# One hybrid decoder layer on one Trainium2 core: values transposed beside their keys, a scaling table through another queue, opening products of ones, three later groups

## The chip, the cores and the metric

The kernel runs on one core of a Trainium2 chip. The metric is device microseconds (us) of one execution, the median of three runs. The engines are TensorE (PE in the profile, its weight loads PEld), VectorE (DVE), ScalarE (ACT), GpSimd (POOL) and SyncE (SP, which only starts transfers here). A matmul engine's clock has two levels, 1.2 and 2.4 GHz.

## What is computed

One step of one layer for 512 new prompt tokens and 8 running sequences of 8 tokens, 576 columns in all, in float32:

```python
h = _rmsnorm(x, norm_mix_g)
proj = jnp.einsum('bld,de->ble', h, w_in)
...
o_dn, S_new = _gated_delta_rule(dq, dkk, dvv, g, beta, S0)      # 8 heads, keys and values of 128
h_ml, C_new, n_new, m_new = _mlstm(mq, mk, mv, ig, logf, C0, n0, m0)   # 4 heads
x = x + jnp.einsum('ble,ed->bld', mix, w_out)
u = jnp.einsum('bld,df->blf', _rmsnorm(x, norm_ffn_g), w_up)
x = x + jnp.einsum('blf,fd->bld', silu(gate) * up, w_down)
```

In the gated delta rule a key's norm scales the key and, in this kernel's form, the value too: `irk` is the square root of the sum of the key's squares, and a value, transposed to have tokens on partitions, is multiplied by it. The triangular system of each chunk is solved through the inverse of a unit triangular matrix.

## The kernel before

**Dense products.** All of w_in, w_out, w_up and w_down is multiplied in split precision: a weight tile and an activation tile are each split into a high and a low part (`wh`, `wl`, `ah`, `al`), and each 128x128 weight block takes three products (`three`, L196 to L201) in two halves of 288 columns, six matmuls. `dense` walks 16 blocks k of one output tile; after each k it calls `tick`. Weights come as 512 KB tiles of eight blocks (`raw`), cast to `wh` by ACT (L120) and subtracted to `wl` by DVE (L121).

**Small products.** The heads' work consists of generators. `spawn` puts one on a list, `tick` advances each that is due, and `yield n` makes it wait n ticks, so a small product stands between two k of a dense product. PE's order is the order in which the program is written; the other engines' order is set by a scheduler with priorities. The heads run in the order m0 d0 d1 m1 d2 d3 m2 d4 d5 d6 d7 m3 (d: gated delta, m: mLSTM). Five heads (d1, d3, d5, d6, d7) do their key products while the delta head before them runs its recurrence (L751 to L771) and its sample part (`dn_sample`); d0, d2 and d4 do theirs alone.

**PSUM for small products.** `psr()` (L111) gives one of four banks. A bank is taken again when everything that reads the products in it has run.

**One delta head** (`dn_head`, L660). Keys are transposed (L683) and ACT squares each of four chunks with a running sum (L686) and scales it (L687); a second bank holds the samples' transposed keys (L689) and two small products (L690, L691). POOL turns the sums into `irk` with a power (L696). One tick later come the keys' products (L710), one tick later keys by queries (L721), one tick later the values' transposes (L732) and, in a bank of their own, the samples' values (L737), scaled by `irk` on ACT (L735, L738). Then `inverse` runs on (L918 to L965), and the recurrence.

**The start** (`startup`, L360). `g1`, 16 scaling columns (8 KB), is fetched through POOL's queue; x comes as 16 tiles of 288 KB through SP's queue, with weight tiles after tiles 1, 7 and 15. ACT makes `ah` from x and g1 (L384), DVE makes `al` (L385). `gate_rows` (L429) computes gates in products between the dense ones (L446, L455, L476, L480, L520).

**Line numbers in the change.** A line of the kernel before stands at +1 in the changed kernel up to L372, at +5 up to L679, at +6 for L683 to L691, at +7 for L702, at +8 for L710 to L723, at +7 for L732 and L735, and at +4 from L751 on. L698 and L711 there are the transposes of samples' values and its scaling, which were L737 and L738.

Of the kernel before, what the change touches and what calls it, by code (L numbers as in the profile page):

```python
# [12 lines left out]
AF = mybir.ActivationFunctionType  # L13
ALU = mybir.AluOpType

P = 128
D = 2048
KT = 16
# [20 lines left out]
OPA = 1600  # L39
YI = 8  # L40
YJ = 20


G1, G2, G3, CW, DG, MG, FW, FBI, GB, AL, M0, NPAR = 0, 16, 32, 48, 144, 145, 153, 417, 505, 506, 507, 515
# [22 lines left out]
class Layer:  # L67
# [292 lines left out]
    def startup(self):  # L360
        nc, I = self.nc, self.I
        self.par = self.cp.tile([P, NPAR], F32, tag="par", name="par")
        g1 = self.cp.tile([P, KT], F32, tag="g1", name="g1")
        nc.gpsimd.dma_start(out=g1, in_=I["par"][:, G1:G1 + KT])
        self.ones = self.cp.tile([P, P], F32, tag="ones", name="ones")
        nc.vector.memset(self.ones, 1.0)
        nc.scalar.activation(self.rstd_tile()[:, 0:1], self.ones[:, 0:1], AF.Copy)
        self.eps6 = self.cp.tile([P, 1], F32, tag="eps6", name="eps6")
        nc.vector.memset(self.eps6, EPS)
        self.epsh = self.cp.tile([P, 1], F32, tag="epsh", name="epsh")  # L370
        nc.vector.memset(self.epsh, EPS * EPS * P)

        self.xh, self.xl, self.xs = [], [], []
        self.gw = self.r(shape=[P, KT, 32])
        acts = [self.new_act(k) for k in reversed(range(KT))][::-1]
        for k in range(KT):
            x = self.r()
            self.xs.append(x)
            nc.sync.dma_start(out=x, in_=I["xT"][k])
            if k in (1, 7, 15):  # L380
                self.load_unit()
            hi, lo = acts[k]
            g = g1[:, k:k + 1]
            nc.scalar.activation(hi, x, AF.Copy, scale=g)  # L384
            nc.vector.scalar_tensor_tensor(out=lo, in0=x, scalar=g, in1=hi.bitcast(F32), op0=ALU.mult, op1=ALU.subtract)  # L385
            self.xh.append(hi)
            self.xl.append(lo)
        for k in range(0, KT, 4):
            self.gate_weights(k, g1)
        nc.sync.dma_start(out=self.par, in_=I["par"])  # L390
# [38 lines left out]
    def gate_rows(self):  # L429
        nc, I, O = self.nc, self.I, self.O  # L430
        V, A, Pl, mm = nc.vector, nc.scalar, nc.gpsimd, nc.tensor.matmul
# [34 lines left out]
        for j, (s, _) in enumerate(quarters):  # L466
            Pl.tensor_copy(there[s, :, 0:8], self.ident[s, s].rearrange("p (g w) -> p g w", g=4))
            Pl.tensor_copy(back[s, :, j], self.ident[s, 32 * j:32 * j + 8].unsqueeze(1).to_broadcast([32, 4, 8]))
            n, v = ((3, 0.5), (5, 1.0), (4, 1.0), (5, 1.0))[j]
# [40 lines left out]
        for s, t in quarters:  # L510
            V.scalar_tensor_tensor(out=t5[s, t], in0=y[s], scalar=cq[s, 4:5], in1=val[s], op0=ALU.mult, op1=ALU.add)
        edge.__exit__(None, None, None)
        yield 12
        R1, R2, R3 = self.r(), self.r(), self.r()
        for t in (R1, R2, R3):
            Pl.memset(t, 0.0)
# [68 lines left out]
        for i, t in enumerate((R1, R2, R3)):  # L585
            pr = self.psr()
            pv = pr.rearrange("p (c g w) -> p c g w", c=4, g=4)
# [72 lines left out]
    def dn_head(self, h, q, k, v, sz):  # L660
        nc, I, O = self.nc, self.I, self.O
        V, A, Pl, mm = nc.vector, nc.scalar, nc.gpsimd, nc.tensor.matmul
        sl4 = slice(SEQ, NT)
# [13 lines left out]
        Pl.memset(ss[64:128, 4:5], 1.0)  # L677
        kd = self.r()
        kds = self.t1([64, P], "kds", 2)  # L679
        pk = self.psr()  # L680
        for c in range(NCH):
            sl, n = self.blk(c)
# [5 lines left out]
        pk = self.psr()  # L688
        nc.tensor.transpose(pk[0:64, 0:P], k[:, sl4], self.ident)  # L689
        mm(pk[0:64, P:P + 64], k[:, sl4], k[:, sl4], start=True, stop=True)  # L690
        mm(pk[0:64, P + 64:2 * P], k[:, sl4], q[:, sl4], start=True, stop=True)  # L691
        A.activation(kds, pk[0:64, 0:P], AF.Square, accum_out=ss[0:64, 4:5])
        A.activation(kds, pk[0:64, 0:P], AF.Copy, scale=self.col(2, 4, 1, h))
        V.tensor_scalar(out=ss, in0=ss, scalar1=EPS, scalar2=None, op0=ALU.add)
        irk, cj = self.sm(5, "irk"), self.sm(5, "cj")
# [5 lines left out]
        U, KQ = self.r(), em  # L701
        V.scalar_tensor_tensor(out=U[0:64, sl4], in0=pk[0:64, P:P + 64], scalar=cjc(4), in1=em[0:64, sl4], op0=ALU.mult, op1=ALU.mult)  # L702
        V.tensor_tensor(out=KQ[0:64, sl4], in0=pk[0:64, P + 64:2 * P], in1=em[0:64, sl4], op=ALU.mult)
        yield 1


# [7 lines left out]
        res = []  # L714
        inv = self.inverse(U, res, 0)
        next(inv)
        yield 1
        pr = self.psr()
        for c in range(NCH):
            sl, n = self.blk(c)  # L720
# [4 lines left out]


        vs = self.r()
        vss = self.t1([64, P], "vss", 2)
        pv = self.psr()
        for c in range(NCH):  # L730
            sl, n = self.blk(c)
# [1 line left out]
        for c in range(NCH):  # L733
            sl, n = self.blk(c)
            A.activation(vs[:, sl], pv[:, sl], AF.Copy, scale=irk[:, c:c + 1])  # L735
        pv = self.psr()
        nc.tensor.transpose(pv[0:64, 0:P], v[:, sl4], self.ident)  # L737
        A.activation(vss, pv[0:64, 0:P], AF.Copy, scale=irk[0:64, 4:5])  # L738

        yield YI  # L740
        yield from inv
# [111 lines left out]
    def inverse(self, U, res, more):  # L853
# [44 lines left out]
        def masked(i):  # L898
            m = U if i == len(LV) - 1 else self.r()
            Pl.tensor_tensor(out=c4(m), in0=c4(U), in1=self.bc4(self.con[:, C_LV + P * i:C_LV + P * i + P]), op=ALU.mult)  # L900
            return m

        m = masked(0)
        yield YJ + more
        self.tc.cur_priority -= PR
# [166 lines left out]
    def ml_sample(self, h, caug, kws, sT, gl, finish):  # L1072
        nc, O = self.nc, self.O
        V, A, Pl, mm = nc.vector, nc.scalar, nc.gpsimd, nc.tensor.matmul
        sl = slice(SEQ, NT)
        yield 2
        qc = self.r(shape=[P, 2, 257])
        for g in range(2):
            pr = self.psr()
            for j in range(4):  # L1080
                mm(pr[32 * j:32 * j + 32, 0:257], self.qim[:, 4 * g + j], caug[g][:, j], start=True, stop=True)
            A.copy(qc[:, g], pr[:, 0:257])
        yield 2
        pn = self.psr()
        mm(pn[0:64, 0:257], sT[0:64, sl], self.vas, start=True, stop=False)
        for g in range(2):
            mm(pn[32 * g:32 * g + 32, 0:257], self.pick[:, 0], qc[:, g], start=False, stop=True)
        fin = self.spawn(finish(pn, 4))
        bmk = self.con[0:64, C_BM:C_BM + NB]
        yield 4  # L1090
        pm = self.psr()
        mm(pm[:, 0:NB], kws, bmk, start=True, stop=True)
        for b in range(NB):
            n1 = caug[b // 4][:, b % 4, 256:257]
            V.scalar_tensor_tensor(out=n1, in0=n1, scalar=gl[:, 4 + b:5 + b], in1=pm[:, b:b + 1], op0=ALU.mult, op1=ALU.add)
        kp = self.pack(kws, P, "kp", ("hhl", "hhl"))
        vp = self.pack(self.vas, 256, "vp", ("hlh", "lhh"))
        for g in range(4):
            vm = self.masked_rows(vp, g // 2, g % 2 * 2, 2)
            yield W  # L1100
            pr = self.psr()
            mm(pr, kp[:, g // 2], vm, start=True, stop=True)
            for i in range(2):
                b = 2 * g + i
                cc = caug[b // 4][:, b % 4, 0:256]
                V.scalar_tensor_tensor(out=cc, in0=cc, scalar=gl[:, 4 + b:5 + b], in1=pr[:, 256 * i:256 * i + 256], op0=ALU.mult, op1=ALU.add)
        for g in range(2):
            self.later(6, O["sC"][h, g], caug[g])
        while not fin[3]:
            yield 1  # L1110
# [628 lines left out]
```

## Time and profile before

| | us |
|---|---|
| median of three runs | 2661.8 (2661.02 to 2662.45) |
| the profiled execution | 2660.97 |
| its span | 2659.2 |
| PE busy | 2628.2, 99% of the span |
| DVE, ACT, POOL busy | 2057.7, 1083.3, 461.6 |
| first matmul starts | 8.50 |
| share of PE in the chain that ended last | 96% |

The span is the time from the first to the last instruction in the profile; some 1.8 us of the execution lie around it. "Idle before" in a row is the time in which an engine had nothing running, with what ended it behind the arrow. A busy PE is not a PE at its peak, since matmuls overlap: the distance from one start to the next is what counts.

### The profile page before, as it was taken

To read this page: it belongs to the slowest core of one execution; us is meant where nothing else is said; L and a number is where in the kernel's file an instruction comes from. 1 tells how busy PE (TensorE), PEld (TensorE's weight loads), DVE (VectorE), ACT (ScalarE), POOL (GpSimd) and SP (SyncE) were. 2 spreads that over 40 slices of the span, in tenths; PEclk is the share of its full clock that TensorE was granted. 3 is DMA by queue.
4 is the path that set the end of the run, shared out by engine and by line. 5 is a ranking of instruction groups with operands and counts; after the bars stand their busy time and mean duration, and the time that the engine had idled before them with its cause. 6 is when DMAs were issued, how large, how long until landed. Compare 5 with 4: busy or idle time off the path is not lost.

```text
span 2659.2 us, 49165 instructions
## 1 busy us (share of the span) xinstructions
PE 2628.2 (99%) x20061; PEld 2584.9 (97%) x20061; DVE 2057.7 (77%) x3448; ACT 1083.3 (41%) x1697; POOL 461.6 (17%) x670
## 2 busy tenths in 40 slices
PE   8999999999999999999999999999999999999998
PEld 8999999999999999999999999999999999999997
DVE  6676666667765455599999999999999998988656
ACT  5333433434434333244444444444444443434224
POOL 2222322322322001111212222222222200000001
PEclk9999999999999999999999999999999999999999
DMA  5242322422323434343333333333333463342332
GB/s 206 83 126 87 130 84 78 131 86 85 98 85 106 154 121 135 129 137 114 109 109 109 109 108 108 106 108 107 108 108 109 133 231 90 119 137 71 123 98 100
DMA packets 112682, 304.05 MB, mean 114 GB/s; under 512 B 21928, under 2 KB 28216, under 8 KB 112456
## 3 DMA queue, kind: packets, MB, share of 16 engines
q1 hardware_dynamic: 108616, 292.20, 34.2%
q0 software_dynamic: 1600, 6.35, 0.7%
q8 instruction: 157, 2.57, 0.4%
q10 hardware_dynamic: 2240, 2.36, 0.2%
q14 instruction: 69, 0.57, 0.1%
HBM read 262.44 MB, written 38.42 MB: 113 GB/s over the span
## 4 chain that ended last, share of the span: by engine, by line
PE 96%; DVE 2%; ACT 1%; issue 0%; POOL 0%; DMA 0%; DVEq 0%; POOLq 0%
PE pd L200 38%; PE pr L1358 33%; PE pd L1358 13%; PE pr L200 4%; PE pr L1588 1%; DVE r L1623 0%; PE pr L918 0%; PE pr L258 0%; DVE wl L121 0%; PE pr L721 0%; PE pr L758 0%; ACT r L686 0%; PE pr L930 0%; PE pr L1055 0%; ACT r L687 0%
## 5 line engine op out<-in xcount | busy, mean ns | idle before, releaser
L120 ACT CAST wh<-raw 128x1024 fp32r<-128x1024 f32 (+1 forms) x392 | 403.2, 1029 | 732.2 <-PE pd L200 391.6
L1358 PE MATMUL pr<-bh,wl 128*128 128x288 f32 x2248 | 663.3, 295 | 0.9 <-DVE wl L121 0.9
L1358 PE MATMUL pr<-bh,wh 128*128 128x288 f32 x2248 | 663.4, 295 | 0.3 <-ACT wh L120 0.3
L1358 PE MATMUL pr<-bl,wh 128*128 128x288 f32 x2248 | 663.3, 295 | 0.0
L121 DVE TENSOR_TENSOR wl<-raw,wh 128x1024 fp32r<-128x1024 f32 (+1 forms) x392 | 471.3, 1202 | 109.6 <-ACT wh L120 105.5
L200 PE MATMUL pd<-ah,wh 128*128 128x288 f32 x2304 | 512.9, 304 | 8.5 <-ACT wh L120 8.5
L200 PE MATMUL pd<-al,wh 128*128 128x288 f32 x2304 | 492.9, 295 | 0.0
L200 PE MATMUL pd<-ah,wl 128*128 128x288 f32 x2304 | 491.3, 294 | 0.0
L1358 PEld LDWEIGHTS pr<-bh,wl 128*128 128x128 f32 x2248 | 423.0, 188 | 1.9 <-DVE wl L121 1.9
L1358 PEld LDWEIGHTS pr<-bh,wh 128*128 128x128 f32 x2248 | 422.6, 188 | 0.5 <-ACT wh L120 0.5
L1358 PEld LDWEIGHTS pr<-bl,wh 128*128 128x128 f32 x2248 | 422.9, 188 | 0.1
L200 PEld LDWEIGHTS pd<-ah,wh 128*128 128x128 f32 x2304 | 367.1, 188 | 21.0 <-ACT wh L120 8.5
L200 PEld LDWEIGHTS pd<-ah,wl 128*128 128x128 f32 x2304 | 368.8, 188 | 0.3 <-DVE wl L121 0.3
L200 PEld LDWEIGHTS pd<-al,wh 128*128 128x128 f32 x2304 | 368.1, 188 | 0.0
L120 ACT CAST wh<-s 128x1024 fp32r<-128x1024 f32 (+1 forms) x180 | 178.8, 993 | 364.5 <-DVE s L1323 138.4
L1358 PE MATMUL pd<-bh,wl 128*128 128x288 f32 x888 | 262.1, 295 | 0.6 <-DVE wl L121 0.6
L1358 PE MATMUL pd<-bl,wh 128*128 128x288 f32 x888 | 262.2, 295 | 0.0
L1358 PE MATMUL pd<-bh,wh 128*128 128x288 f32 x888 | 262.0, 295 | 0.0
L1240 POOL COPY fst<-r 128x18 f32<-128x18 f32 x88 | 97.6, 1109 | 678.8 <-DVE r L1396 678.8
L121 DVE TENSOR_TENSOR wl<-s,wh 128x1024 fp32r<-128x1024 f32 (+1 forms) x180 | 206.5, 1147 | 6.8 <-ACT wh L120 2.2
L1358 PEld LDWEIGHTS pd<-bh,wl 128*128 128x128 f32 x888 | 167.1, 188 | 0.9 <-DVE wl L121 0.9
L1358 PEld LDWEIGHTS pd<-bl,wh 128*128 128x128 f32 x888 | 167.1, 188 | 0.0
(420 smaller groups left out, 3736.1 us busy)
## 6 DMA issues: line engine op xcount, KB each, us to landing
raw<-in_w_up SPq DMA_DIRECT2D x176, 512.0 KB
raw<-in_w_in SPq DMA_DIRECT2D x112, 512.0 KB
raw<-in_w_down SPq DMA_DIRECT2D x40, 512.0 KB
raw<-in_w_out SPq DMA_DIRECT2D x32, 512.0 KB
raw<-in_w_down SPq DMA_DIRECT2D x40, 384.0 KB
hid<-r SPq DMA_DIRECT2D x44, 288.0 KB
r<-hid SPq DMA_DIRECT2D x40, 288.0 KB
r<-in_xT SPq DMA_DIRECT2D x32, 288.0 KB
```

The source lines that it names most:

```text
L120: self.last_split = (nc.scalar.copy(hi, src), nc.vector.tensor_tensor(out=lo, in0=src, in1=hi.bitcast(F32), op=ALU.subtract))
L121: nc.vector.tensor_tensor(out=lo, in0=src, in1=hi.bitcast(F32), op=ALU.subtract))
L200: mm(outs[hf], w, x[:, hf * HALF:(hf + 1) * HALF], start=first and i == 0, stop=last and i == 2)
L1240: nc.gpsimd.tensor_copy(f, rb[:, 512:602].rearrange("p (b w) -> p b w", b=9)[:, :, 0:2])
L1358: mm(out, w[:, ks], x[:, sl], start=k == 0 and i == 0, stop=k == nk - 1 and i == 2)
L1588: mm(pr[:, 0:n], w[:, ks], acts[kk][:, a * NT + sl.start:a * NT + sl.stop], start=kk == 0 and i == 0, stop=kk == FB - 1 and i == 2)
```

## The change

It has four parts. The opening products: 18 matmuls of a 128x128 tile of ones with itself, whose result nobody reads, stand first on PE. The scaling columns' transfer goes from POOL's queue to ACT's. The samples' values are transposed into the bank of the samples' keys, behind L691, and scaled by ACT once `irk` is there; the bank of their own goes away. Three groups stand later in ticks: L520 by two, L721 (and what follows in its head) by one, L1092 (and what follows in `ml_sample`) by one.

```diff
+NW = 18
...
-        nc.gpsimd.dma_start(out=g1, in_=I["par"][:, G1:G1 + KT])
+        nc.scalar.dma_start(out=g1, in_=I["par"][:, G1:G1 + KT])
...
+        pw = self.psr()
+        for _ in range(NW):
+            nc.tensor.matmul(pw[:, 0:P], self.ones, self.ones, start=True, stop=True)
...
-        yield 12
+        yield 14
         R1, R2, R3 = self.r(), self.r(), self.r()
...
+        vss = self.t1([64, P], "vss", 2)
         pk = self.psr()
...
         mm(pk[0:64, P + 64:2 * P], k[:, sl4], q[:, sl4], start=True, stop=True)
+        nc.tensor.transpose(pk[0:64, 2 * P:3 * P], v[:, sl4], self.ident)
...
         V.tensor_tensor(out=KQ[0:64, sl4], in0=pk[0:64, P + 64:2 * P], in1=em[0:64, sl4], op=ALU.mult)
+        A.activation(vss, pk[0:64, 2 * P:3 * P], AF.Copy, scale=irk[0:64, 4:5])
         yield 1
...
         next(inv)
-        yield 1
+        yield 2
         pr = self.psr()
...
-        pv = self.psr()
-        nc.tensor.transpose(pv[0:64, 0:P], v[:, sl4], self.ident)
-        A.activation(vss, pv[0:64, 0:P], AF.Copy, scale=irk[0:64, 4:5])
...
         bmk = self.con[0:64, C_BM:C_BM + NB]
-        yield 4
+        yield 5
```

PE in head d1, beside the recurrence of d0. Before (a line of dots stands for dense products, and between L689 and L710 for L690 and L691 too; `con` is the identity, r_2100 the key, r_1941 the query, r_2243 the value):

```order
L832 MATMUL pr_2528<-vss_1910,Xs_1876 64x128
L683 MATMUL pr_2553<-con,r_2100 128x128 x4
L689 MATMUL pr_2566<-con,r_2100 64x128
...
L710 MATMUL pr_2588<-r_2100 128x128 x4
...
L762 MATMUL pr_2619<-r_1909,r_1828 128x128
L764 MATMUL pr_2619<-r_1744,S_2455 128x128
L765 MATMUL pr_2619<-r_1746,r_1909 128x128
L721 MATMUL pr_2626<-r_1941,r_2100 128x128 x4
...
L839 MATMUL pr_2639<-r_1746,vss_1910 128x64
L732 MATMUL pr_2646<-con,r_2243 128x128 x4
L737 MATMUL pr_2655<-con,r_2243 64x128
```

The same place in the changed kernel (r_2118 the key, r_1959 the query, r_2261 the value):

```order
L689 MATMUL pr_2551<-con,r_2118 128x128 x4
L695 MATMUL pr_2564<-con,r_2118 64x128
...
L698 MATMUL pr_2564<-con,r_2261 64x128
...
L718 MATMUL pr_2588<-r_2118 128x128 x4
L836 MATMUL pr_2613<-vss_1849,Xs_1898 64x128
...
L766 MATMUL pr_2646<-r_1937,r_1847 128x128
L768 MATMUL pr_2646<-r_1758,S_2479 128x128
L769 MATMUL pr_2646<-r_1760,r_1937 128x128
L729 MATMUL pr_2653<-r_1959,r_2118 128x128 x4
...
L739 MATMUL pr_2667<-con,r_2261 128x128 x4
L843 MATMUL pr_2676<-r_1760,vss_1849 128x64
```

L737 has gone into the keys' group as L698. L721, now L729, stands two k of the dense product behind L718 where there was one between L710 and it, still in one group with the recurrence's three products, and the sample product L832, now L836, has gone from ahead of the keys' transposes to behind L718. In the w_in part the dense products are left for small ones at 268 places, where there were 247: groups of two heads that stood between the same two k now often stand a k apart.

ACT at the same place. Before (left out under the dots: more rows of L686, L687, L692, L693 and two L797):

```order
L833 ACTIVATE vss_1910<-pr_2528,cj_1851 64x128
L797 CAST vp_2538<-vss_1910 32x128 x4
L686 ACTIVATE r_2551,ss_2549<-pr_2553 128x128
...
L687 ACTIVATE r_2551<-pr_2553,cols 128x128
L797 CAST kp_3336<-kds_2552 32x128 x2
L771 COPY r_1744<-pr_2619 128x128
L723 ACTIVATE r_1941<-r_1941 128x576
L842 COPY r_1744<-pr_2639 128x64
L735 ACTIVATE r_2644<-pr_2646,irk_2573 128x128 x4
L738 ACTIVATE vss_2645<-pr_2655,irk_2573 64x128
```

In the changed kernel:

```order
L692 ACTIVATE r_2548,ss_2546<-pr_2551 128x128
...
L693 ACTIVATE r_2548<-pr_2551,cols 128x128
L837 ACTIVATE vss_1849<-pr_2613,cj_1872 64x128
L801 CAST kp_3359<-kds_2549 32x128
L801 CAST vp_2623<-vss_1849 32x128 x4
L801 CAST kp_3359<-kds_2549 32x128 x2
L711 ACTIVATE vss_2550<-pr_2564,irk_2572 64x128
L731 ACTIVATE r_1959<-r_1959 128x576
L775 COPY r_1758<-pr_2646 128x128
L742 ACTIVATE r_2666<-pr_2667,irk_2572 128x128 x4
```

The sample's scaling and its casts (L833 and L797, now L837 and L801) have gone from ahead of the eight instructions on the keys to behind them, and L738, now L711, stands ahead of L771 and L735. On POOL the power (L696, now L703) stood behind two L806 and now stands ahead of them.

## Rows read from the trace of the kernel before

**Rows 1.** The page's part 1: busy us of each engine, share of the span, instructions.

```profile
PE 2628.2 (99%) x20061; PEld 2584.9 (97%) x20061; DVE 2057.7 (77%) x3448; ACT 1083.3 (41%) x1697; POOL 461.6 (17%) x670
```

**Rows 2.** Waits on PE: line, what it waited for, us in total, times, longest.

```profile
PE pd L200 <- ACT wh L120: 8.5, 1, 8.5
PE pr L721 <- ACT r L687: 3.8, 5, 0.8
...
PE pr L737 <- POOL r L866: 0.9, 2, 0.5
...
PE pr L1092 <- DVE hn L1040: 0.7, 2, 0.4
PE pr L520 <- DVE r L511: 0.7, 1, 0.7
...
PE pr L737 <- DVE r L703: 0.4, 1, 0.4
```

**Rows 3.** Timeline of the start: start, us, engine, line, operation, idle before.

```profile
0.84 0.17 DVE L366 MEMSET ones<- 128x128 f32 x1 [0.84 <-PEq L1715]
...
1.52 0.68 POOL L364 DMA_DIRECT2D g<-in_par  x1
...
6.07 1.44 ACT L384 ACTIVATE ah<-r,g 128x576 fp32r<-128x576 f32 x2 [3.83 <-DMA g<-in_par]
```

**Rows 4.** Timeline of PE from its first matmul on; x2 are two matmuls.

```profile
10.41 0.68 PE L200 MATMUL pd<-ah,wh 128*128 128x288 f32 x2
10.89 0.68 PE L200 MATMUL pd<-al,wh 128*128 128x288 f32 x2
...
12.89 0.42 PE L200 MATMUL pd<-ah,wh 128*128 128x288 f32 x2
...
17.12 0.43 PE L200 MATMUL pd<-al,wh 128*128 128x288 f32 x2
```

**Rows 5.** SP's queue: the issue that waited for the second weight tile, and its wait.

```profile
12.28 0.33 SPq L379 DMA_DIRECT2D r<-in_xT  x1
...
SPq L379 <- DMA raw<-in_w_in: 1.0, 1, 1.0
```

**Rows 6.** Timeline of ACT and DVE at the second weight tile and behind it.

```profile
12.37 1.04 ACT L120 CAST wh<-raw 128x1024 fp32r<-128x1024 f32 x1
...
14.00 1.22 DVE L121 TENSOR_TENSOR wl<-raw,wh 128x1024 fp32r<-128x1024 f32 x1
...
15.13 5.92 DVE L385 SCALAR_TENSOR_TENSOR al<-r,g,ah 128x576 fp32r<-128x576 f32 x8
```

**Rows 7.** Timeline of PE in head d1.

```profile
209.22 0.43 PE L832 MATMUL pr<-vss,Xs 64*64 64x128 f32 x2
...
211.56 1.05 PE L710 MATMUL pr<-r 128*128 128x128 f32 x8
212.36 0.51 PE L200 MATMUL pd<-ah,wh 128*128 128x288 f32 x2
212.72 0.42 PE L200 MATMUL pd<-al,wh 128*128 128x288 f32 x2
...
213.24 0.38 PE L762 MATMUL pr<-r,r 128*128 128x128 f32 x2
...
214.82 1.16 PE L721 MATMUL pr<-r,r 128*128 128x128 f32 x8 [0.76 <-ACT r L687]
```

**Rows 8.** Timeline of ACT and POOL in the same stretch.

```profile
210.84 1.04 POOL L806 TENSOR_TENSOR vm<-vp,con 96x512 fp32r<-96x512 f32 x1 [3.72 <-ACT vp L797]
...
211.36 0.28 ACT L686 ACTIVATE r<-pr 128x128 f32<-128x128 f32 x1
...
214.34 1.18 POOL L696 TENSOR_TENSOR irk<-ss,half 128x5 f32<-128x5 f32 x1 [1.13 <-DVE ss L694]
214.40 0.37 ACT L687 ACTIVATE r<-pr,cols 128x128 f32<-128x128 f32 x1
214.79 0.60 ACT L797 CAST kp<-kds 32x128 fp32r<-32x128 f32 x2
```

More of the change, by code (lines that the diff above doesn't have):

```diff
@@ L727, in dn_head @@
         vs = self.r()
-        vss = self.t1([64, P], "vss", 2)
         pv = self.psr()
```

## The prediction

> **What bounds the kernel.** I read the page's busy times first. PE is busy for 2628.2 of the span's 2659.2 us, so only three things can move the end: time in which PE stands, time in which it works at half rate, and instructions added to it [rows 1]. DVE is next with 77% and cannot set the end over the whole span, only in single stretches. So I went to the waits on PE. The reader is to see there that 8.5 us lie ahead of the first matmul and that the other named waits are short and come from few lines: L721 stands five times for ACT's L687, 3.8 us in all; L737 three times, 0.9 and 0.4 us; L1092 twice, 0.7; L520 once, 0.7 [rows 2]. Those four make 6.5 us, and they are the lines that the change moves. Then the timelines of the start: ACT's first `ah` waits 3.83 us for the scaling columns, which POOL had issued at 1.52 [rows 3]. PE begins at 8.50 with a pair of matmuls every 0.48 us (10.41 to 10.89); from 12.89 to 17.12 sixteen pairs take 0.264 us each [rows 4]. 576 columns in 0.48 us are 1.2 GHz; the second pace belongs to 2.4. (The column of granted clock says full speed throughout, so I take the spacing.)
>
> **The opening products and the scaling columns.** What does an earlier and faster start bring? Nine pairs start between 8.50 and 12.89, 4.39 us, where nine at the later pace take 2.4: half rate costs 2.0 us. But PE has to be fed. The ninth block of the first dense product needs the second weight tile and `al` of the ninth x tile. The issue that waits for that weight tile does so for 1.0 us and goes out at 12.28, so the tile lands just before [rows 5]; ACT casts it from 12.37 to 13.41, and nothing in the change brings that forward, since x and weights come in the same order through SP's queue. DVE took `wl` from 14.00, with `al` behind it from 15.13, 0.74 us apiece (5.92 for eight) [rows 6]. In the changed kernel DVE is free sooner and can start `wl` at 13.41: 1.22 and 0.74 later, at 15.4, PE can have the second pair of the ninth block. Before, it had it at 17.12 [rows 4]. From there PE is slower (0.79 a block) than DVE (0.74). So the start gives 17.1 less 15.4, **1.7 us**, if PE gets there in time: 25 pairs at 0.264 lie ahead, so the first one must start by 8.75 at full rate.
>
> Does it? `ones` is ready at 1.01 [rows 3]. Four products of the same kind (L710, eight records) take 0.80 us, 211.56 to 212.36 [rows 7], so 18 take 3.6 us at full rate, or 6.6 at 0.48/0.264 of that: they end between 4.6 and 7.6. The scaling columns need not even come sooner, since 8.50 is early enough; their move only makes room. The issue itself goes ahead of ACT's first work, in a stretch in which ACT waited 3.83 us [rows 3], and POOL loses 0.68 us of work that PE does not wait for; both at nothing.
>
> The clock is the uncertain part. In this trace it rose after 4.4 us of PE's work, which lies inside the time of the ones; by that row the start gives 1.7 and the sum is 7.2. The Trainium skill (TensorE: Matmul & The Clock Gate, Part 1) says that one kernel had 6, 11 or 14 slow products at its start, depending on the run; no run here shows that yet. By that rule the rise may come only after the ones have ended.
>
> If it does, the first real product starts at about 7.6 and the first nine pairs are slow: the ninth block's second pair is at 7.6 + 25 x 0.264 + 2.0 = 16.2, a start worth 0.9 and a sum of 6.4. The bounds of this term: nothing, since even twice 3.6 us of ones ends at 8.2, ahead of the 8.50 of before, which excludes a loss; and 2.9, if DVE's `wl` did not stand ahead of that `al` (1.22). I take 1.7, since the rows give DVE that order.
>
> **L520, two ticks later.** It waited 0.7 us for DVE's L511 [rows 2]. A tick is one block, three pairs, 0.79 us; two are 1.58, twice the wait. What follows in that generator, three later groups and four small transfers on SP's queue, comes 1.6 us later too; the heads wait for them, but the dense products go on meanwhile and the last small product stands some 88 blocks (70 us) ahead of the w_out part, so that costs nothing. Gain **0.7**.
>
> **L1092, one tick later**: it waited twice 0.4 us for its bank; 0.79 covers it. Gain **0.7**, bounds 0 and 1.0 (L1044 behind it had 0.3 of its own).
>
> **Samples' values beside their keys.** The transpose is moved, not removed: the same PE time. What goes is its bank and the wait for it, 0.9 and 0.4 [rows 2]: **1.3**. In return the keys' bank is held until ACT's L711, which needs `irk`. The next to take that bank in a paired head is L732; see below whether it waits.
>
> **L721, one tick later.** Head d1: L721 could have gone at 214.06 and went at 214.82, when the last L687 (214.40, 0.37) had read the bank [rows 7, 8]. One tick alone makes 214.85. In the new order, though, L762 takes that bank, ahead of L721: it stood at 213.24, and comes 0.79 (the tick), 0.2 (the transpose) and 0.4 (L832, which now lies between) later, 214.6 [rows 7]. That would be 0.1 short, but ACT no longer does the sample's scaling and four casts ahead of the keys: at 0.30 a cast (0.60 for two) and 0.3 for the scaling it reaches L687's last 1.2 to 1.5 us sooner, at about 213.4 [rows 8]. So L762 does not wait. Then L732: L762 at 214.6, 0.82 to L721, 0.92 for it (214.82 to 215.74 as before), a block of 0.9: 217.2. L711 behind it: last L687 at 213.4, scaling and seven casts 2.4, L711 0.4: 216.2; the power (214.34, 1.18) comes 1.2 sooner, at 214.3, and does not end last. The cover is **1 us**, and the gain all five waits, **3.8**, bounds 0 and 3.8.
>
> **What the moves add.** PE leaves the dense products at 268 places instead of 247. Behind L710 the first pair takes 0.36 us instead of 0.264 [rows 7], so a place costs at most 0.10; a bound below is nothing, where a group hides its switch. No row has a place by itself, so I take the middle, 0.05: 21 places, **-1.0**, bounds -2.1 and 0.
>
> **Sum.** 1.7 + 0.7 + 0.7 + 1.3 + 3.8 - 1.0 = 7.2 us. The profiled execution took 2660.97, 0.8 under the median of 2661.8; 2660.97 - 7.2 = 2653.8 there, so 2654.6 for the median. A measurement of this kernel can tell about 0.2%, 5.3 us, from no change: the border is 2656.5.
>
> **Rivals.**
> *The ones do not raise the clock in time.* For it: one trace cannot tell how the clock's rise varies. Against: 4.4 us of work were enough there. The sum is 6.4, 2655.4. Chance 0.13.
> *The wait moves on to the bank's next user.* L762 takes the keys' bank, L732 the bank held by L711, and ACT's order behind L687 is longer by L833 and four casts. If ACT is 1.8 us later than I have it, 0.8 us past its cover, the five waits of 0.76 come back under other lines and 7.2 - 3.8 = 3.4 remain: 2658.4. For it: the cover of 1 us is made of sums of rows. Against: ACT is busy 41%. Chance 0.18.
> *Slower.* The same place, but L711 late by more: ACT takes its queue in order, L711 stands behind eight casts and scalings that wait on PE and DVE in turn, and L771 and L735 of the recurrence stand behind it. At 3.5 us late, 2.5 past the cover in five heads, it costs 12.5: 2654.6 + 12.5 = 2667.1. It turns into a loss from 1.4 us past the cover on (7.2/5). For it: POOL's power has already waited 1.13 us for DVE in this stretch [rows 8]. Against: in the new order the power stands ahead of the two L806 (1.04 each) it stood behind. Chance 0.05.
>
> **How the numbers follow.** The forecast of 2654.6 has 0.62, the rivals 0.13, 0.18 and 0.05; 0.02 is for what I do not see. From the forecast, 0.55 lies below the border and 0.07 above (an L721 wait or two left, or switches at 0.10); of the first rival 0.10 lies below. Faster 0.65, within 0.2% 0.30, slower 0.05. The range: below, the term of switches at nothing and L1044's wait gone (1.3 more) and 0.7 for the spread of the runs shown: 2652.6; a start near its upper bound is left to the outer tenths. Above, the second rival: 2658.5. With the slower rival, what lies below and the unseen, under 0.2 is left out.
>
> **What would show it.** Right: 18 products on PE from about 1.1; the pairs at 0.264 from the first one; the ninth block's second pair near 15.4; no row of waits for L737's successor, L729 (L721 before) or L525 (L520 before); PE's idle time down by some 6 us besides the start. Wrong: a row of 0.48 us pairs after 7; new waits of PE for ACT's L693 or L711 near L766 or L739 in the five paired heads; a first dense product that ends no sooner.

## The result, and the profile of the changed kernel

The changed kernel takes 2668.5 us, median of 11 runs, where the kernel before took 2662.0 beside it: a ratio of 1.0025 with a 95% interval of 1.0016 to 1.0033. It is 6.5 us slower; the forecast was 7.2 us faster, with a range up to 2658.5. The profiled execution of the changed kernel took 2666.8, its span 2665.0 (2659.2 before).

**The page first** (busy time of PE, then the chain that ended last).

```profile
PE 2634.2 (99%) x20097; PEld 2590.5 (97%) x20097; DVE 2067.2 (78%) x3448; ACT 1081.0 (41%) x1697; POOL 457.4 (17%) x669
...
PE 88%; DVE 7%; issue 2%; DMA 1%; ACT 1%; POOL 1%; SPq 0%; DVEq 0%; POOLq 0%; ACTq 0%
```

PE's busy time grew by 6.0 us against [rows 1], but the opening products alone are 6.7 of it. What is new stands in the chain: PE had 96% of it and DVE 2%; now PE has 88% and DVE 7%.

**The start** did what was forecast. On PE (start, us, engine, line, operation, idle before):

```profile
1.06 6.67 PE L377 MATMUL pr<-ones 128*128 128x128 f32 x36 [1.06 <-DVE epsh L372]
7.48 0.51 PE L201 MATMUL pd<-ah,wh 128*128 128x288 f32 x2
...
8.96 0.43 PE L201 MATMUL pd<-ah,wh 128*128 128x288 f32 x2
9.22 0.43 PE L201 MATMUL pd<-al,wh 128*128 128x288 f32 x2
...
15.01 0.54 PE L201 MATMUL pd<-al,wh 128*128 128x288 f32 x2
```

and on ACT and DVE:

```profile
3.86 1.44 ACT L389 ACTIVATE ah<-r,g 128x576 fp32r<-128x576 f32 x2 [1.18 <-DMA g<-in_par]
...
11.92 1.05 ACT L121 CAST wh<-raw 128x1024 fp32r<-128x1024 f32 x1 [0.51 <-DMA raw<-in_w_in]
...
13.00 1.23 DVE L122 TENSOR_TENSOR wl<-raw,wh 128x1024 fp32r<-128x1024 f32 x1
```

ACT's first `ah` starts at 3.86 where it had started at 6.07 [rows 3]. The ones fill PE from 1.06 to 7.48, 6.4 us; their 36 records start 0.21 us apart at first and 0.11 apart from 6.1 on, so PE changes to its full pace while they run. Behind them no real pair is at the slow pace: the pairs follow each other at 0.26 us, but for two waits, and the ninth block's second pair stands at 15.01. Before it stood at 17.12 [rows 4]: 2.1 us.

That sets one trace against one trace, and the start is not the same in each. Over all profiled executions, that pair lies between 17.1 and 19.2 in the five without the ones, which begin with 7 to 12 pairs more than 0.35 us apart, and between 14.9 and 16.4 in the nine with them; there the ones change pace between 4.7 and 7.1, always before they end. The means are 2.7 us apart.

**The waits on PE** (line, what it waited for, us in total, times, longest):

```profile
PE pr L762 <- DVE rr L757: 4.1, 5, 0.9
PE pr L850 <- DVE r L730: 3.7, 4, 1.3
PE pr L922 <- DVE r L915: 3.1, 2, 1.5
PE pd L201 <- DVE wl L122: 2.3, 2, 2.0
...
PE pr L766 <- DVE hn L1044: 1.2, 2, 0.6
```

None of the four old lines is left: the 6.5 us of [rows 2] at L721, L737, L1092 and L520 are gone. In their place stand 14 us of waits for one engine, DVE, 10.9 of them in the delta heads (L762, L850, L922). The sum of these two traces closes: PE's gaps of over 50 ns behind the first 20 us went from 10.9 to 17.4 us (summed over all its rows), +6.5; the start gave -2.1; the span grew by 5.8, so 1.4 is left for all else, the 21 more interruptions of the dense products among it.

**Head d1, where L850 waits for KQ's bank.** PE:

```profile
205.36 0.60 PE L689 MATMUL pr<-con,r 128*128 128x128 f32 x4
...
207.31 1.05 PE L718 MATMUL pr<-r 128*128 128x128 f32 x8
208.29 0.43 PE L836 MATMUL pr<-vss,Xs 64*64 64x128 f32 x2
...
218.01 0.47 PE L850 MATMUL pr<-vm,kp 96*128 96x512 f32 x1 [1.12 <-DVE r L730]
```

ACT, POOL and DVE in the same stretch:

```profile
209.54 1.26 ACT L801 CAST vp<-vss 32x128 fp32r<-32x128 f32 x4
...
208.81 1.27 POOL L703 TENSOR_TENSOR irk<-ss,half 128x5 f32<-128x5 f32 x1 [5.94 <-DVE ss L701]
...
213.37 1.04 POOL L810 TENSOR_TENSOR vm<-vp,con 96x512 fp32r<-96x512 f32 x1
214.70 1.04 POOL L810 TENSOR_TENSOR vm<-vp,con 96x512 fp32r<-96x512 f32 x1 [0.29 <-DVE vp L803]
215.70 1.28 POOL L904 TENSOR_TENSOR r<-r,con 128x512 f32<-128x512 f32 x1
...
213.47 1.08 DVE L803 TENSOR_TENSOR vp<-vss,vp 32x128 fp32r<-32x128 f32 x1
...
214.85 2.42 DVE L877 TENSOR_TENSOR r<-r 128x256 f32<-128x256 f32 x1
217.19 0.68 DVE L730 TENSOR_TENSOR r<-pr,r 128x512 f32<-128x512 f32 x1
```

The sample product L836 stands behind the next head's key group (L689 to L718), and so do its casts, and the two masks that POOL makes from them (L810). Before, the masks ran at 210.84 [rows 8] and 212.16, around the keys' products at 211.56 [rows 7]; now they come 6.1 and 7.4 us behind those. There they meet the inverse's additions on DVE: L877, 128x256, starts beside the second L810, lasts 2.42 us through it and through L904 behind it, and ends 0.29 after L904. KQ (L730) stands behind it on DVE, and PE's L850 waits for KQ's bank. The same place before:

```profile
211.05 0.97 DVE L799 TENSOR_TENSOR vp<-vss,vp 32x128 fp32r<-32x128 f32 x1 [0.36 <-ACT vp L797]
...
212.16 1.04 POOL L806 TENSOR_TENSOR vm<-vp,con 96x512 fp32r<-96x512 f32 x1 [0.28 <-ACT kds L692]
...
218.84 1.28 POOL L900 TENSOR_TENSOR r<-r,con 128x512 f32<-128x512 f32 x1
...
218.84 0.67 DVE L722 TENSOR_TENSOR r<-pr,r 128x512 f32<-128x512 f32 x1
219.44 1.29 DVE L873 TENSOR_TENSOR r<-r 128x256 f32<-128x256 f32 x2
```

Here L722 ran ahead of the long addition; that is the first of the two in the last row and took 0.97 us beside L900 alone. In the unpaired heads, with no POOL instruction beside it, the same 128x256 addition takes 0.40 (three times in either kernel). In d0 before, where it is the longest of the line's three (shortest, middle and longest in ns):

```profile
L873 DVE TENSOR_TENSOR r<-r x3: 174/293/404, 153.2 to 155.7; 64x32 f32<-64x32 f32 x1, 128x256 f32<-128x256 f32 x1, 128x128 f32<-128x128 f32 x1
```

In the changed kernel it takes 2.42 us in d1, d3 and d7, beside two masks, and 1.17 in d5 and d6, where only the second L810 lies beside it. The two waits at L922, 1.5 us each, are in d5 and d6.

### The profile page after: what moved, and what is told of

Read it like the earlier page. It is cut to its first block, busy times and chain, and to the rows that moved or that the text cites. A ratio compares the mean times of both kernels' runs of the same rounds, so it can differ in the third digit from the quotient of the medians.

```text
span 2665.0 us, 49244 instructions
## 1 busy us (share of the span) xinstructions
PE 2634.2 (99%) x20097; PEld 2590.5 (97%) x20097; DVE 2067.2 (78%) x3448; ACT 1081.0 (41%) x1697; POOL 457.4 (17%) x669
## 4 chain that ended last, share of the span: by engine, by line
PE 88%; DVE 7%; issue 2%; DMA 1%; ACT 1%; POOL 1%; SPq 0%; DVEq 0%; POOLq 0%; ACTq 0%
PE pr L1362 33%; PE pd L201 32%; PE pd L1362 13%; PE pr L201 3%; PE pr L1592 1%; DVE wl L122 1%; DVE r L625 0%; DVE bl L122 0%; DVE r L877 0%; DVE vp L803 0%; DVE r L894 0%; DVE r L896 0%; ACT wh L121 0%; DVE r L1627 0%; DMA r<-ud 0%
## 5 line engine op out<-in xcount | busy, mean ns | idle before, releaser
L122 DVE TENSOR_TENSOR wl<-raw,wh 128x1024 fp32r<-128x1024 f32 (+1 forms) x392 | 472.0, 1204 | 95.6 <-ACT wh L121 90.6
L122 DVE TENSOR_TENSOR wl<-s,wh 128x1024 fp32r<-128x1024 f32 (+1 forms) x180 | 206.5, 1147 | 6.3 <-ACT wh L121 1.1
```

The lines of the kernel that those rows point to most:

```text
L122: nc.vector.tensor_tensor(out=lo, in0=src, in1=hi.bitcast(F32), op=ALU.subtract))
```

## The experiments

Theory A: the tick at the keys-by-queries products (yield 2 before L729) is the cost, since the rest of its head slips against the next. Theory B: the merged bank is the cost. Theory C: it takes both. Later A1 and A2 part: A1 says that the slip of the sample part does it, A2 that the products' own lateness does. Each kernel has its own line numbers; I give the counterpart where it isn't plain. Ratios stand to the kernel before on the same chip, five rounds each.

### The start alone

The 18 products of ones and the scaling columns' queue, as in the change, on the kernel before.

> The kernel before with the two parts of the start alone: the 18 products of ones and the scaling columns on ScalarE's queue. Every theory gives the same here: in the profile of the changed kernel the ninth block's second pair stood 2.1 us earlier and no pair ran slowly, so 2.1 us less than before (2659.9 us by a median of 2662.0), the waits in the mixer as before. Were the products of ones to cost something later (another clock, another order), the rest of the kernel would be longer and the gain under 1 us.

Measured: 2659.8 by 2661.4 of before, ratio 0.9993 (0.9985 to 1.0002). 1.7 us less, of the size expected, though the interval holds no change as well.

### The merged bank alone

```diff
+        vss = self.t1([64, P], "vss", 2)
...
         mm(pk[0:64, P + 64:2 * P], k[:, sl4], q[:, sl4], start=True, stop=True)
+        nc.tensor.transpose(pk[0:64, 2 * P:3 * P], v[:, sl4], self.ident)
...
+        A.activation(vss, pk[0:64, 2 * P:3 * P], AF.Copy, scale=irk[0:64, 4:5])
         yield 1
...
-        vss = self.t1([64, P], "vss", 2)
...
-        pv = self.psr()
-        nc.tensor.transpose(pv[0:64, 0:P], v[:, sl4], self.ident)
-        A.activation(vss, pv[0:64, 0:P], AF.Copy, scale=irk[0:64, 4:5])
```

> The kernel before with the transposition of the sample's values beside the keys alone (one bank and one wait fewer, the scaling of them earlier on ScalarE). Theory A (the tick that puts the key-by-query products later is what costs): the wait of 1.3 us in three heads goes, 0 to 1.3 us less than before, no wait for DVE. Theory B (the merged bank is held until the scaling is read from it, and this puts the heads late): the waits for L757's, L730's and L915's counterparts on DVE appear here, and the time is 6 to 10 us more than before.

Measured: 2662.6 by 2661.4, ratio 1.0005 (0.9996 to 1.0014). Theory B falls: none of the waits of the paired heads appears. But the gain isn't there either. On PE (L917 is the inverse's first product, L918 before, in the unpaired heads d0, d2 and d4):

```profile
PE pr L724 <- ACT r L688: 3.6, 5, 0.7
PE pr L917 <- issue: 2.3, 3, 0.8
```

and on DVE and POOL in d0:

```profile
176.51 1.80 DVE L908 TENSOR_TENSOR r<-cx,con 128x512 f32<-128x512 f32 x1
...
178.36 0.69 DVE L910 STREAM_TRANSPOSE r<-r 128x512 f32<-128x512 f32 x1
...
175.98 1.77 POOL L899 TENSOR_TENSOR r<-r,con 128x512 f32<-128x512 f32 x1
```

The 1.3 us at L737 went, and 2.3 came some 25 us on in the same three heads. The profile names no releaser, but L917 starts at 179.16, 0.1 after the transposition it needs. PE came there sooner, and DVE, which runs without a break through this stretch, did not. Part of DVE's time there is due to POOL: L908 lies beside the mask L899, takes 1.80 us and ends 0.55 after it, where its counterpart takes 0.68 with no mask beside it (L913 in d5 of the changed kernel). Those 1.1 us were there before too (1.79); only now PE is early enough to wait for them.

### The tick at the products alone

```diff
         next(inv)
-        yield 1
+        yield 2
```

> The kernel before with the key-by-query products one tick later (yield 2 for yield 1 at L721's group) alone. Theory A: the five waits at L721 (3.8 us) go, and the waits for DVE that the changed kernel shows (some 13 us) come, as the sample part of the head before now lies behind the next head's key group: 8 to 11 us more than before, about 2671 us. Theory B: only the 3.8 us go, about 2658 us. Theory C (it takes two of the parts together): under 4 us more or less than before.

Measured: 2678.0 by 2661.4, ratio 1.0062 (1.0049 to 1.0075). Theory A's direction, and some 6 us more than its upper end; B and C fall. On PE:

```profile
PE pr L839 <- ACT r L771: 9.6, 5, 2.0
PE pr L758 <- DVE rr L753: 6.5, 3, 2.4
```

The five waits at L721 are gone, and the long addition takes up to 2.4 us as in the changed kernel. The largest wait is one that the changed kernel does not have: L839, the sample's next product, wants a bank that ACT's L771 has still to read, and L771 waits for DVE's `S` (L768) behind an addition and a cast's difference that take 1.0 and 1.1 us beside POOL's work (0.17 and 0.28 alone). In the changed kernel L839's counterpart L843 goes at 213.22, ahead of L771's counterpart (214.97), so it takes another bank there; the wait comes at L850 instead, 3.7 us. That the bank that is no longer taken shifts the ring of four is the likely reason, which no run shows by itself. The changed kernel without the start's 2.1 us would be 8.6 above before, where the tick alone is 16.6: beside it the other parts are worth some 8 us, without it next to nothing (the changed kernel with the old tick, below).

### The changed kernel with the old tick there

The change as it is, but `yield 1` before the products.

> The changed kernel with yield 1 again at the key-by-query products, all else as changed. Theory A: 2.1 (start) + 1.3 (the bank) + 0.7 + 0.7 (the two other groups) = 4.8 us less than before, about 2657 us, no waits for DVE in the heads, and the five waits at L721 (3.8 us) back. Theory B: still slower than before, by 6 to 10 us. Theory C: between the two, with part of the waits for DVE left.

Measured: 2658.8 by 2661.4, ratio 0.9990 (0.9981 to 0.9999): Theory A, some 2 us above its number. The waits for DVE in the paired heads are gone. It is short of 2657 mainly by 3.0 us of waits at L922, the inverse's first product, as in the run of the merged bank.

### The products' tick, given back behind them

In the changed kernel, and in the kernel before with `yield 2` at the products:

```diff
-        yield YI
+        yield YI - 1
         yield from inv
```

On the changed kernel:

> The changed kernel, with the tick that the key-by-query products were put later given back behind the values' transpositions (yield YI - 1 there), so that the next head and this head's sample part stand to each other as before. Theory A1 (not the products' own lateness costs, but that the sample part of one head slips by a tick against the next head's key group): the waits for DVE in the paired heads go and those at the products stay away: 2668.5 less 8 to 13 us, 2656 to 2660 us, and at least 2 us under the run with yield 1. Theory A2 (the products' own tick makes KQ late, and with it the bank): the waits for KQ at the sample's state products stay, 3 to 4 us of them, above 2662 us.

Measured: 2657.2 by 2661.5, ratio 0.9983 (0.9974 to 0.9992). On the kernel before:

> The kernel before with the key-by-query products one tick later and the tick given back (yield 2, then yield YI - 1), nothing else. Theory A1: the five waits at L721 (3.8 us) go and nothing comes: about 2657.6 us by a before of 2661.4. Theory A2: some 3 to 10 us more than that. A rival to both: the wait of 0.75 us only moves to the next that wants a bank or ScalarE in the same place (L839 or L732): 2660 to 2661.5 us.

Measured: 2660.8 by 2661.5, ratio 0.9998 (0.9988 to 1.0007). A1 holds in both: the products are as late as in the changed kernel, and neither L850 nor L762 waits; in the first the long addition still takes 1.50 us beside POOL's L904, but KQ has run ahead of it. So the contention is not gone; nothing of weight stands behind it. On PE in the second:

```profile
PE pr L721 <- ACT r L771: 2.5, 5, 0.5
PE pr L918 <- issue: 2.0, 3, 0.7
```

So the rival, that the wait only moves, holds for a good part: of L721's 3.8 us 2.5 stay, now for another reader of the bank (L771 in place of L687), and 2.0 arise at L918.

### KQ ahead of the long addition

```diff
-        V.tensor_tensor(out=KQ[:, 0:SEQ], in0=pr, in1=em[:, 0:SEQ], op=ALU.mult)
+        with self.urgent():
+            V.tensor_tensor(out=KQ[:, 0:SEQ], in0=pr, in1=em[:, 0:SEQ], op=ALU.mult)
```

> The changed kernel, with VectorE's product that reads the key-by-query bank (L730) given precedence, so that in each of the five paired heads it runs ahead of the inverse's long addition (L877, 128x256), which there took 2.42 us beside GpSimd's masks, and 0.65 us elsewhere. If that addition is what holds the bank, the three waits at L850 (3.7 us, 3.5 of them in these heads) go, 2 to 4 us less than the changed kernel (2664.5 to 2666.5 us), and the other waits for DVE (L762, L922, L766) stay. If the bank is held by something else, under 1 us changes.

Measured: 2664.8 by 2661.5, 1.0013 of before (1.0004 to 1.0022): 3.4 us above before, where the changed kernel is 6.5 above, so 3.1 less. No wait at L850 is left (L851 here, where lines stand one later):

```profile
PE pr L763 <- DVE rr L758: 5.7, 8, 0.9
PE pr L923 <- DVE r L916: 3.1, 2, 1.5
```

The other waits stay, and those for `rr` grow, as `rr` too stands behind the addition and PE, no longer held at L850, comes to it sooner. So it was the addition that held the bank. (The 0.65 us of the expectation is half of a row of two additions, 1.29; the long one takes 0.97 there and 0.40 alone.) DVE and POOL in d1:

```profile
214.63 0.68 DVE L731 TENSOR_TENSOR r<-pr,r 128x512 f32<-128x512 f32 x1
215.23 1.82 DVE L878 TENSOR_TENSOR r<-r 128x256 f32<-128x256 f32 x1
...
214.48 1.04 POOL L811 TENSOR_TENSOR vm<-vp,con 96x512 fp32r<-96x512 f32 x1 [0.29 <-DVE vp L804]
215.48 1.28 POOL L905 TENSOR_TENSOR r<-r,con 128x512 f32<-128x512 f32 x1
```

KQ (L731), with one operand in PSUM, takes 0.68 us in the midst of a mask, as everywhere; the addition behind it, both operands in SBUF, ends 0.29 after POOL's last.

### POOL's mask away from the long addition

```diff
+        yield YJ + more
         m = masked(0)
-        yield YJ + more
```

> The changed kernel, with GpSimd's first mask of the inverse (L904) issued later, behind the wait for the diagonal blocks, so that in three of the five paired heads it no longer runs beside VectorE's long addition (L877); the order on TensorE, VectorE and ScalarE stays. If the addition is held by GpSimd's work beside it: it takes 1.17 us there, as in the two heads without that mask, not 2.42 us, so KQ comes 1.25 us earlier, the waits of 1.1 to 1.3 us at L850 in these three heads go, and the time is 3 to 5 us less than the changed kernel's (2663.5 to 2665.5 us). If the addition is slow for another reason: it stays at 2.42 us, and the time within 1 us.

Measured: 2668.4, the changed kernel's time (1.0027 of before, 1.0016 to 1.0038); the profiled execution is the slowest of the seven, 2672.7, so its waits are somewhat longer than usual. Half of it came as expected: the addition takes 1.17 us in all five heads, and of the waits at L850 0.2 us remain. The expected gain was lost elsewhere, and the place shows the cause once more. DVE, POOL and PE in d1, 11 us further on:

```profile
217.95 1.17 DVE L877 TENSOR_TENSOR r<-r 128x256 f32<-128x256 f32 x1
...
228.87 0.21 DVE L894 TENSOR_TENSOR r<-r 40x54 f32<-40x54 f32 x1
229.11 1.28 DVE L896 TENSOR_TENSOR r<-r 40x54 f32<-40x54 f32 x1
...
229.04 1.29 POOL L904 TENSOR_TENSOR r<-r,con 128x512 f32<-128x512 f32 x1
...
232.21 0.49 PE L762 MATMUL pr<-rr,r 128*128 128x128 f32 x2 [1.80 <-DVE rr L757]
```

L904 now meets the inverse's chain of small steps. The one that starts 0.07 after it, 0.21 us otherwise, takes 1.28, and `rr` behind it is late: L762 waits 1.80 here, where in the changed kernel it waited 0.68. At L762 7.1 us stand in this run (4.1), at L922 4.2 (3.3). POOL's work was put beside another DVE instruction, and that one stands as near to PE. In d0 the same happened: the wide multiplication at the inverse's end (L913) now takes 0.68, but the 64x64 one behind it lies beside L904 and takes 1.31 instead of 0.21, and L922 waits 0.6 us there (0.2 in the changed kernel).

### All but the merged bank, with the tick given back

The start, gates at 14, normalizer's groups at 5, `yield 2` and `YI - 1`.

> All of the change but the merged bank of the values, and with the tick given back: start, gates at 14, the normalizer's groups at 5, products at 2 and YI - 1. If the parts add up: 2661.4 - 2.1 - 0.7 - 0.7 - 3.8 = 2654.1 us. If the orders on DVE shift again as they did with the merged bank (waits at the inverse's products, 2.3 us there), 2656 to 2658 us.

Measured: 2658.5 by 2661.5, ratio 0.9989 (0.9980 to 0.9998). The parts do not add up: waits of 2.5 us at the products and 2.0 at the inverse's first product are about what is missing from 2654.1.

### Two ticks, both given back

In the changed kernel `yield 3` at the products and `yield YI - 2` behind them.

> The changed kernel with the products two ticks later than before and both ticks given back (yield 3, then yield YI - 2). In the run with one tick given back 2.4 us of waits were left at the products (0.5 us in each of five heads, for ScalarE's copy of L775). If the bank is all that they want there, these go: 2 to 2.5 us under 2657.2 us, about 2655 us. If KQ's product on VectorE then comes too late for the next user of its bank or for the sample part, waits at L843 or L850 take their place: 2657 us or more.

Measured: 2655.5 by 2661.9, ratio 0.9975 (0.9966 to 0.9984): faster than both kernels by 6.4 and 13 us. The products wait no more; 1.6 us arise at L762 in two heads, less than the 2.4 that went:

```profile
PE pr L922 <- issue: 2.7, 3, 1.2
PE pr L762 <- DVE rr L757: 1.6, 2, 1.3
```

### Start, gates and normalizer's groups

The change without the merged bank and without the products' tick.

> The kernel before with the start, the gates two ticks later and the normalizer's groups one tick later, neither the merged bank nor the products. By the prediction's terms: 2.1 + 0.7 + 0.7 = 3.5 us less, about 2658 us. By what the runs since showed: the 0.7 us at the gates go, those at the normalizer's groups return as waits of 0.4 us at L1044's products for hn: 2.1 + 0.7 = 2.8 us less, about 2658.6 us, and the waits of 0.75 us at L721 stay.

Measured: 2659.2 by 2661.9, ratio 0.9990 (0.9981 to 0.9999). On PE (L726 is L721, L1049 is L1044 of before):

```profile
PE pr L726 <- ACT r L692: 3.7, 5, 0.7
...
PE pr L1049 <- DVE hn L1045: 0.8, 2, 0.4
```

There is no row for the gates' group any more, nor for the normalizer's; but where the latter waited 0.7 us, the next product now waits 0.8. That part of the change moved a wait by one line; in the changed kernel it is the 1.2 us at L766.

### The slip without the products' tick

The kernel before with `yield YI + 1` for `yield YI` and nothing else.

> The kernel before with one tick more behind the values' transpositions (yield YI + 1) and nothing else: the products stand at their old tick behind the keys', but the sample part of a head slips by a tick against the next head's key group, as it does in the changed kernel. Theory A1 (that slip is the cost): about as slow as the run with the products' tick alone, 10 to 18 us more than before, with waits at L758 for rr and at L839, and VectorE's long addition (L873) at over 2 us in three heads. Theory A2 (the cost needs the products to be late): under 3 us more than before.

Measured: 2678.5 by 2662.0, ratio 1.0061 (1.0047 to 1.0075). A1, without the products being any later behind their keys:

```profile
PE pr L839 <- DVE r L722: 9.7, 5, 2.0
...
PE pr L758 <- DVE rr L753: 4.7, 3, 2.2
```

That closes the square: neither 2662; products late with the tick given back -0.7; slip alone +16.5; both +16.6 us. What slips is all that stands behind the values' transposes, the recurrence as well as the sample part; no run moves the sample part by itself.

## Why the prediction was wrong, point by point

**The failed step** is L721's: "The cover is 1 us, and the gain all five waits, 3.8". The five waits did go. But a `yield` lengthens the whole generator, and what follows in its head, the sample part above all, came a tick later against the next head, which had not moved. That the sample product and its casts now stood behind the next head's keys was seen; it was followed on ACT, POOL and PE and there found harmless. It was not followed on DVE, whose order was read only for the start. Behind the casts stand two masks on POOL, and these came to lie beside DVE's additions, with KQ, `rr` and the state of the recurrence queued behind them. By the runs the slip alone costs 16.5 us. In the changed kernel, 6.5 us above before with the tick and 2.6 below without it, the term that was to gain 3.8 lost 9.1; all the other terms together, 3.4 by the forecast, made 2.6.

**What spoke against the slower rival was a sign of the cause.** The power's place ahead of the two L806 on POOL was counted as a relief. It was one for `irk`. But it also meant that the masks had fallen back, from 0.7 ahead of the keys' products to 6.1 behind them, and what that would meet was not asked. The slower rival's own mechanism did not happen: L711 ran at 211.63, its successor L731 at 212.09, and no PE row waits for either. That its 2667.1 lies near 2668.5 is chance.

**Start, 1.7**: right in its mechanism, and in its size as far as can be told; 2.1 in the changed kernel's trace, 1.7 in the run of it alone, whose interval holds no change as well. The ones took 6.4 us, within the 3.6 to 6.6 reckoned, and from DVE's `wl` to the ninth block's second pair it is the forecast's 2.0 (13.00 to 15.01). But the prediction held that nothing would bring the cast of the second weight tile forward from 12.37, and it ran at 11.92: that is the 0.4 between 2.1 and 1.7, and it is less than what differs between executions: the cast lies between 12.4 and 13.9 in the five traces without the ones and between 11.8 and 13.3 in the nine with them. The rival of a late clock did not come true in any of the nine, by 0.8 us at the least. The Trainium skill (TensorE: Matmul & The Clock Gate, Part 1) says that the number of slow products at the start differs from run to run; the traces agree, with 7 to 12 slow pairs at the front of the five without the ones.

**L520, 0.7**: the wait is gone, and nothing took its place in the run without the heads' parts. **L1092, 0.7**: the wait is gone, and 0.8 us stand at the next product instead (1.2 in the changed kernel, at L766); nothing gained, the term's lower bound. **L737's bank, 1.3**: nothing gained, 1.1 us more in the run alone, with no change inside its interval; PE reached DVE's inverse sooner and waited there. Here the prediction gave no lower bound under the gain, and asked only who takes the bank next, not which engine the head runs into next. **Interruptions, -1.0**: no run shows them apart; 1.4 us is what the account above leaves for them and all else.

**DVE against POOL.** In the changed kernel the long addition took 2.42 us beside L810 and L904, in the mask run 1.17 beside L810 alone, and before 0.97 beside L900. It ended 0.3 us after POOL's last in each, while KQ, which reads PSUM, kept its 0.68 beside a mask (0.69 at most in any run). The Trainium skill (SBUF — State Buffer, section "SBUF: two separate sides") says that a VectorE instruction with two inputs in SBUF and a GpSimd instruction that reads SBUF share a pair of ports, that whichever starts first holds it for its whole length, and that the other blocks fully. The traces agree: DVE instructions that take 0.21, 0.40 and 0.68 us alone end 0.08, 0.28 and 0.55 us after the mask beside them (the 64x64 multiplication, the long addition and the 128x512 multiplication), so each did nearly all its work when POOL was done. That section says nothing of two POOL instructions in a row; here the addition did not get in between L810 and L904.

**What stays open**: how much of the cost is this contention. The run with KQ ahead of the addition takes 3.1 us of it away. The waits for `rr`, and those at L922 in d5 and d6, where the difference of a weight tile (L122, 1.21 us) has come between the multiplication and the transposition on DVE, are put down to DVE's later and longer work from the traces alone. So are the waits at L922 in the three unpaired heads (2.0 to 3.0 us in the runs that save PE time there): the mask beside the wide multiplication costs DVE 1.1 us in each, but no run takes that mask out of DVE's way.

## What to carry to other kernels

A wait that is moved by a tick moves all that its generator does later: give the tick back behind the moved group, and compare the order of every engine, not only of those on which the old wait stood. Where an engine is nearly always busy, the wait that ends is often only the first in a row of several, and the gain is what the next one leaves; test it by the part alone before adding parts up. And when POOL's work moves, look at what DVE does in the same microsecond.

## What was not expected of the hardware

One POOL instruction of 1.29 us made a DVE step of 0.21 us take 1.28, and two end to end made an addition of 0.40 take 2.42; an instruction with one operand in PSUM kept its time beside the same work. So which of DVE's instructions stands beside a mask decided more here than how much work either engine has: POOL is busy for 17% of the span.
